# Ten of 32 modulation sums, and the row they are multiplied with, formed in the first stage of a transformer block

## The chip, the cores and the metric

The kernel runs on one core of a Trainium2 chip. Its engines work side by side, each through its own list of instructions in order: PE multiplies matrices, DVE (VectorE) and ACT (ScalarE) work on vectors, POOL (GpSimd) does a little, and SP (SyncE) issues the transfers, which 16 DMA engines carry out. The metric is the time of the program on the device in microseconds, the median of several runs.

## The reference

One layer of a block over 256 tokens of width 1024, in float32. A conditioning vector c modulates it; a mixer with three branches and gates follows, then a mixture of 32 experts:

```python
cond = jax.nn.silu(c)
mod = cond @ w_ada[layer] + b_ada[layer]              # 1024 -> 6 * 1024
sh_m, sc_m, g_m, sh_f, sc_f, g_f = [m[:, None, :] for m in jnp.split(mod, 6, axis=-1)]
h = rms_norm(x, norm_mix[layer]) * (1.0 + sc_m) + sh_m
x = x + g_m * hybrid_mixer(h, ...)    # h @ w_in, then recurrence, two attentions, 3 x 1024 gates, w_branch, w_out
h = rms_norm(x, norm_ffn[layer]) * (1.0 + sc_f) + sh_f
x = x + g_f * moe_ffn(h, ...)         # router, top 4 of 32 experts, 1024 -> 2048 -> 1024 each
```

The first two of the six parts of mod (sc_m, sh_m) are needed at once, to form h. The other four (g_m, sc_f, sh_f, g_f) are needed only after the branches have been merged.

## The kernel before, in words

*First stage* (`branches`, up to the loop over d). h is formed in eight blocks d of 128 columns, and each block is multiplied with its rows of the weights for v, q, k and the window's k and v as soon as it is there. A product in float32 is made of three matmuls (`mm3`): a weight tile is split by ACT into a rounded part `whi` and by DVE into the rest `wlo`, h into `h[0]` (the cast, L273) and `h[1]` (the subtraction, L274). The modulation of h (`ada_rows`) is formed in groups of blocks, {0}, {1}, {2, 3}, {4, 5}, {6, 7}: PE multiplies silu(c) with weight columns (L246), ACT copies the sums (`rd`, L251), PE picks them into columns (L253), DVE adds the bias (`mod`, L255), multiplies with the norm's gain (`A`, L257) and forms `hd` (L268), from which the casts make h.

*The 32 late sums* (`ada`, L207). Columns 16 to 47 of mod are formed on DVE instead: `csb` is a tile with silu(c) in every row (`row_tile`, eight small matmuls with the name silu), and one instruction multiplies a weight tile `wada` of 128 x 1024 (512 KB) with it and sums along the row; a second, tiny one writes the sum. `ada(i)` makes two sums, and i runs from 8 to 23. Before, `ada(8)` and `ada(9)` stand in the loop over the two tiles of `gr`, the rest in the loop over the 12 tiles of the gates, as the list `ADA` says.

*Then* come normalised q and k (`qk_norm`), the bias table of both attentions (`bias_tiles`: a matmul, an addition `relb` (L282), a store `scr` to DRAM by POOL (L284) and three loads `tz` (L288) that spread it over the partitions), the differential attention `diff` (scores L437 on PE, L439 on DVE reading `tz`), the window attention `swa`, the recurrence `lru`, and 12 weight tiles of gates (`proj_ch`), each split in two halves.

*Then* `merge`, `project`, `route`, and the experts (`moe`), whose 400 MB of weights (`w1h`, `w2h`) pass through a ring of buffers (`order`, `slot`, `blocks`); SP issues a load when the buffer's last reader is done.

*Order.* Only the first instructions stand as written. The rest is put in order by a scheduler that may move instructions of one engine past each other where no data forbids it; the order that it makes is fixed in the program. Sums of late calls therefore stand among the instructions of earlier stages.

Of the kernel before, what the change touches and what calls it, by code (L numbers as in the profile page):

```python
# [10 lines left out]
F32 = mybir.dt.float32  # L11
F32R = mybir.dt.float32r
# [8 lines left out]
T, D, NE, FF = 256, 1024, 32, 1024  # L21
# [8 lines left out]
    + [(s, d) for d in range(8) for s in (4, 3)] + [(5, d) for d in range(8)]  # L30


ADA = [[10], [11], [12, 13], [14, 15], [16, 17], [18, 19], [20, 21], [22, 23], [], [], [], []]


C_C, C_NM, C_NF, C_CW, C_CB, C_BA, C_BX, C_LAM = 0, 8, 16, 24, 40, 44, 48, 52
# [8 lines left out]
class Kernel:  # L45
# [148 lines left out]
    def ada_load(self, i, first=False):  # L194
        ws = []
        for j in range(2):
            ws.append(self.p4("wada") if first else self.p4p.tile([128, D], F32, name="wada", tag="wada", bufs=2))
            src = self.a["wad0"][i] if first else self.a["wada"][i - 8]
            self.nc.sync.dma_start(out=ws[j], in_=src[:, j * D:(j + 1) * D])
        return ws  # L200

    def ada(self, i, ws=None):

        nc = self.nc
        for j, w in enumerate(ws or self.ada_load(i)):
            c = 2 * i + j
            nc.vector.tensor_tensor_reduce(out=w, in0=w, in1=self.csb, scale=0.5, scalar=self.col(C_BADA + c),  # L207
                                           op0=ALU.mult, op1=ALU.add, accum_out=self.mod[:, c:c + 1])
# [339 lines left out]
    def mixer(self):  # L548
        nc, tc, a = self.nc, self.tc, self.a
        with ExitStack() as st:  # L550
            self.dram = st.enter_context(tc.tile_pool(name="dram", bufs=1, space=DRAM))
            self.mix = mix = self.pool(st, "mix", 1)
            self.wsp = self.pool(st, "wsp", 3)
            self.h = [self.keep.tile([128, 8, T], F32R, name=f"h{i}", tag=f"h{i}") for i in range(2)]
            with ExitStack() as s3:
                mid = self.pool(s3, "mid", 1)
                br = [[mid.tile([128, 4, T], F32R, name=f"br{n}{i}") for i in range(2)] for n in range(3)]
                gl = [mid.tile([128, 4, T], F32, name=f"gl{b}") for b in range(6)]
                with ExitStack() as s2:
                    self.early = self.pool(s2, "early", 1, "right")  # L560
                    self.mw = self.pool(s2, "mw", 2, "right")
                    self.aw = self.pool(s2, "aw", 2, "right")
                    self.p4p = self.pool(s2, "p4", 9, "right")
                    self.branches(br, gl)
                self.keep2 = self.pool(self.ctx, "keep2", 1, "right")
                wp2 = self.pool(self.ctx, "wp2", 1, "right")
                self.order += [(wp2, f"v{i}", 2) for i in range(3)]
                self.merge(br, gl)
            self.wst = ExitStack()
            wp3 = self.pool(self.wst, "wp3", 1, "right")  # L570
            self.project(st)
            o = {s[1]: s for s in self.order}
            self.order = [(wp3, f"u{i}", 2) for i in range(3)] + [o["v0"], o["v1"], (wp3, "u3", 1)] \
                + [o[t] for t in ("w1", "w2", "w0", "v2")]
            self.half = None
            self.route()

    def branches(self, br, gl):
# [26 lines left out]
        for d in range(8):  # L605
            if d:
                wt = self.load(a["wqkv"][d])
                hi, lo = self.split(wt[:, :1024])
                self.tokens_k(pv, self.h, d, hi[:, :512], lo[:, :512])
                self.tokens_k(pq, self.h, d, hi[:, 512:], lo[:, 512:])  # L610
            g = groups.get(d)
            if g:
                self.ada_rows(g, [self.ada_load(e, first=True) for e in g])
                for e in g:
                    self.h_chunk(gl[e // 4][:, e % 4], e)
            hi, lo = self.split(wt[:, 1024:]) if d else (hi2, lo2)
            self.tokens_k(pk, self.h, d, hi[:, :512], lo[:, :512])
            for t in range(2):
                tt = slice(t * 128, (t + 1) * 128)
                self.mm3(pkv[:, t * 256:(t + 1) * 256], (self.h[0][:, d, tt], self.h[1][:, d, tt]),  # L620
                         (hi[:, 512:], lo[:, 512:]), d + t == 0, d + t == 8)
        dv = self.p4("dv").rearrange("p (t m) -> p t m", t=2)
        for t, p in enumerate(pv):
            nc.scalar.copy(dv[:, t], p)
        self.csb = self.row_tile("silu", self.sc, self.mix)
        xr = self.p4("xr", 4 * (T + 3)).rearrange("p (c m) -> p c m", c=4)
        nc.vector.memset(xr[:, :, 0:3], 0.0)
        nc.scalar.copy(xr[:, 0:2, 3:], self.proj_ch(0))
# [13 lines left out]
        sq = tok4("sqT")  # L642
        for t, p in enumerate(self.proj([self.po(), self.po()], self.h, a["wsq"])):
            self.qk_norm(p, 512, self.gains[:, 1:2], sq, t)
        self.diff(dq, dk, dv, br[1])
        self.lru_prepare()
        gr = tok4("gr")
        for i in range(2):
            nc.scalar.copy(gr[:, 2 * i:2 * i + 2], self.proj_ch(2 + i))
            self.ada(8 + i)  # L650
        self.swa(sq, sk, sv, br[2])
        self.lru(xr, gr, br[0])
        for b in range(6):
            for i in range(2):
                nc.scalar.activation(gl[b][:, 2 * i:2 * i + 2], self.proj_ch(4 + 2 * b + i), AF.Tanh, scale=0.5)
                for j in ADA[2 * b + i]:
                    self.ada(j)
# [604 lines left out]
```

## Time and profile before

| | |
|---|---|
| median of 3 runs | 1236.62 us (1233.0 to 1238.64) |
| profiled execution | 1236.15 us, of it 1234.4 us span from the first to the last instruction |
| PE busy | 1130.4 us (92%) |
| DVE busy | 452.1 us (37%) |
| ACT busy | 253.8 us (21%) |
| moved by DMA | 470.70 MB, 381 GB/s over the span |
| the 32 late sums (L207) | 40.8 us of DVE, 1277 ns each |

A share of the whole span averages over stages with different limits, so it says little of one stage; the stretches do. A matmul's recorded duration overlaps the next one's, and its pace is read from the distance of two starts. The profile puts a time in square brackets where an engine was idle before an instruction, with what ended the idle time.

### The profile page before, as it was taken

Reading aid. Unit: us, or ns where it says so; the run is one execution under the profiler, and the core shown is the slowest. Engines: PE = TensorE matmul, PEld = TensorE weight load, DVE = VectorE, ACT = ScalarE, POOL = GpSimd, SP = SyncE. Lnnn points to the kernel's source line nnn. Section 1 sums busy time; section 2 is a strip of 40 time slices with the busy share of each in tenths; the row PEclk is TensorE's granted clock in tenths of the full one; section 3 lists DMA queues with packets and bytes.
Section 4 is the critical chain, followed back from the end, with each engine's and each line's share of the span. In section 5 each row is a group of like instructions: output and inputs, shape, how many; then the busy total and the mean of one; then the engine's idle time right before and its main releaser. Section 6 shows DMA issues by size and latency. Waiting matters only on the chain.

```text
span 1234.4 us, 13920 instructions
## 1 busy us (share of the span) xinstructions
PE 1130.4 (92%) x5719; PEld 550.9 (45%) x5720; DVE 452.1 (37%) x889; ACT 253.8 (21%) x441; POOL 11.0 (1%) x19
## 2 busy tenths in 40 slices
PE   6998999998988999998989798989897989898987
PEld 4787889985333334332423242324233323333223
DVE  3578878973123231231314032303131222122232
ACT  4475658443101011010101010101000000100100
POOL 0000000000010000000000000000000000000000
PEclk9999999998989999999999999989999999999999
DMA  9678567795999999999999999999999999999996
GB/s 373 246 254 319 181 207 257 307 375 202 425 419 425 425 426 423 427 425 426 423 428 426 425 425 425 429 424 425 425 426 426 424 426 424 428 425 425 425 402 223
DMA packets 54862, 470.70 MB, mean 381 GB/s; under 512 B 6064, under 2 KB 8168, under 8 KB 21256
## 3 DMA queue, kind: packets, MB, share of 16 engines
q1 hardware_dynamic: 53256, 466.93, 92.0%
q0 software_dynamic: 528, 1.72, 0.4%
q10 hardware_dynamic: 1008, 1.09, 0.3%
q8 instruction: 47, 0.77, 0.3%
q14 instruction: 23, 0.19, 0.0%
HBM read 468.65 MB, written 1.07 MB: 381 GB/s over the span
## 4 chain that ended last, share of the span: by engine, by line
PE 59%; DMA 35%; DVE 4%; ACT 1%; issue 1%; SPq 0%; DVEq 0%; ACTq 0%
DMA wt<-w2h 19%; DMA wt<-w1h 14%; PE po L961 11%; PE mm L961 10%; PE ps L981 9%; PE ps L994 4%; PE ps L921 3%; PE mm L125 3%; PE mm L124 3%; PE mm L126 3%; PE po L124 1%; PE po L125 1%; PE po L126 1%; PE ps L888 1%; PE ps L437 1%; DVE wlo L109 1%
## 5 line engine op out<-in xcount | busy, mean ns | idle before, releaser
L961 PE MATMUL po<-wt,xT 128*64 128x512 f32 x992 | 336.4, 601 | 27.3 <-DMA wt<-w1h 27.2
L961 PE MATMUL mm<-wt,xT 128*64 128x512 f32 x992 | 331.9, 596 | 0.0
L981 PE MATMUL ps<-wt,act 128*64 128x512 f32 x992 | 237.6, 621 | 41.3 <-DMA wt<-w2h 34.6
L987 DVE TENSOR_TENSOR y<-ps,gf 64x512 f32<-64x512 f32 x62 | 42.7, 688 | 353.2 <-PE ps L981 352.5
L961 PEld LDWEIGHTS po<-wt,xT 128*64 128x64 f32 x992 | 88.2, 137 | 167.5 <-issue 112.7
L981 PEld LDWEIGHTS ps<-wt,act 128*64 128x64 f32 x992 | 73.2, 142 | 191.1 <-issue 138.1
L961 PEld LDWEIGHTS mm<-wt,xT 128*64 128x64 f32 x992 | 93.2, 137 | 133.0 <-issue 131.3
L891 DVE TENSOR_TENSOR g<-ps,b1t 128x512 f32<-128x512 f32 x31 | 21.4, 692 | 243.4 <-PE ps L888 243.4
L109 DVE TENSOR_TENSOR wlo<-wt,whi 128x1024 fp32r<-128x1024 f32 x72 | 85.5, 1192 | 23.6 <-ACT whi L117 23.2
L117 ACT CAST whi<-wt 128x1024 fp32r<-128x1024 f32 x72 | 73.3, 1022 | 57.3 <-PE mm L125 21.5
L965 ACT COPY hg<-po 128x512 f32<-128x512 f32 x31 | 18.1, 585 | 301.8 <-PE po L961 254.9
L124 PE MATMUL mm<-h,whi 128*128 128x256 f32 x256 | 73.6, 287 | 0.0
L125 PE MATMUL mm<-h,whi 128*128 128x256 f32 x256 | 73.5, 287 | 0.0
L126 PE MATMUL mm<-h,wlo 128*128 128x256 f32 x256 | 73.0, 285 | 0.0
L994 PE MATMUL ps<-y,swT 128*128 128x512 f32 (+1 forms) x128 | 58.2, 606 | 7.2 <-DVE y L987 7.2
L894 ACT ACTIVATE ps<-g 128x512 f32<-128x512 f32 x31 | 18.6, 601 | 220.6 <-DVE g L892 220.6
L996 DVE TENSOR_TENSOR x<-x,ps 128x512 f32<-128x512 f32 x64 | 43.8, 687 | 18.8 <-PE ps L994 18.8
L125 PEld LDWEIGHTS mm<-h,whi 128*128 128x128 f32 x256 | 48.5, 190 | 2.1 <-issue 1.9
L126 PEld LDWEIGHTS mm<-h,wlo 128*128 128x128 f32 x256 | 48.7, 190 | 1.0 <-issue 1.0
L124 PEld LDWEIGHTS mm<-h,whi 128*128 128x128 f32 x256 | 48.6, 190 | 1.0 <-issue 1.0
L924 ACT ACTIVATE xT<-ps,B,A 128x256 f32<-128x256 f32 x32 | 17.4, 564 | 141.4 <-PE ps L921 141.2
L207 DVE CUSTOM_DVE_ANT_0 wada<-wada,silu,cols 128x1024 f32<-128x1024 f32 x32 | 40.8, 1277 | 6.0 <-DMA wada<-wada 6.0
(342 smaller groups left out, 1097.9 us busy)
## 6 DMA issues: line engine op xcount, KB each, us to landing
wt<-w1h SPq DMA_DIRECT2D x93, 2048.0 KB, 29.5
wt<-w2h SPq DMA_DIRECT2D x47, 2048.0 KB, 29.5
wt<-w1h SPq DMA_DIRECT2D x70, 1024.0 KB, 29.5
wt<-w2h SPq DMA_DIRECT2D x33, 1024.0 KB, 31.0
wt<-wch SPq DMA_DIRECT2D x16, 1024.0 KB, 5.8
wada<-wada SPq DMA_DIRECT2D x32, 512.0 KB, 5.3
wada<-wad SPq DMA_DIRECT2D x16, 512.0 KB, 8.2
wt<-wqkv SPq DMA_DIRECT2D x7, 896.0 KB, 9.3
```

Of the source, the lines that this page charges most:

```text
L109: eng.tensor_tensor(lo, x, hi.bitcast(F32), op=ALU.subtract)
L117: self.nc.scalar.copy(hi, w)
L124: nc.tensor.matmul(out, lhs[0], rhs[0], start=start, stop=False)
L125: nc.tensor.matmul(out, lhs[0], rhs[1], start=False, stop=False)
L126: nc.tensor.matmul(out, lhs[1], rhs[0], start=False, stop=stop)
L207: nc.vector.tensor_tensor_reduce(out=w, in0=w, in1=self.csb, scale=0.5, scalar=self.col(C_BADA + c), op0=ALU.mult, op1=ALU.add, accum_out= ...
L921: nc.tensor.matmul(p[:, i * 256:(i + 1) * 256], self.xs[j][:, t, d * 128:(d + 1) * 128], sel[:, t], start=(t + j == 0), stop=(t + j == 2))
L961: nc.tensor.matmul(p[64 * hf:64 * hf + 64], xT[:, k, i * CAP:(i + 1) * CAP], w[:, (2 * j + hf) * 512:(2 * j + hf + 1) * 512], start=(k == ...
L981: nc.tensor.matmul(py[rows[hf]], act[:, (k % 4) * 2 + k // 4, :], w[:, (2 * i + hf) * 512:(2 * i + hf + 1) * 512], start=(k == 0), stop=(k ...
L987: nc.vector.tensor_mul(self.y[r, hf], py[r], self.gf[r, hf * 512:(hf + 1) * 512])
L994: nc.tensor.matmul(p, swT[r, i, t * 128:(t + 1) * 128], self.y[r, hf], start=True, stop=True)
L996: nc.vector.tensor_add(self.x[:, t, s], self.x[:, t, s], p)
```

## The change

`ada(8)` to `ada(12)`, ten of the 32 sums, are called in the loop of the first stage (`EARLY`: after the first projections of blocks 2, 3, 4, 6 and 7), each with tiles of its own. These tiles (`wadm`) take the memory of gate tiles and branch tiles, which are made only later in the program now. The row `csb` that the sums need is formed at block 1 instead of behind the loop. The other 22 sums are spread over 11 of the 12 gate tiles, two to each; none is left with the tiles of `gr`.

```diff
-ADA = [[10], [11], [12, 13], [14, 15], [16, 17], [18, 19], [20, 21], [22, 23], [], [], [], []]
+ADA = [[13], [14], [15], [16], [17], [18], [19], [20], [21], [22], [23], []]
+EARLY = {2: 8, 3: 9, 4: 10, 6: 11, 7: 12}
...
+    def ada_early(self, i):
+        ws = []
+        for j in range(2):
+            n = 2 * (i - 8) + j
+            ws.append(self.mid.tile([128, D], F32, name="wadm", tag=f"gl{2 + n}" if n < 4 else f"br{n // 2 - 2}{n % 2}"))
+            self.nc.sync.dma_start(out=ws[j], in_=self.a["wada"][i - 8][:, j * D:(j + 1) * D])
+        self.ada(i, ws)
...
-                br = [[mid.tile([128, 4, T], F32R, name=f"br{n}{i}") for i in range(2)] for n in range(3)]
-                gl = [mid.tile([128, 4, T], F32, name=f"gl{b}") for b in range(6)]
+                self.mid = mid
+                br = [[None] * 2 for _ in range(3)]
+                gl = [mid.tile([128, 4, T], F32, name=f"gl{b}") for b in range(2)]
...
+            if d == 1:
+                self.csb = self.row_tile("silu", self.sc, self.mix)
+            if d in EARLY:
+                self.ada_early(EARLY[d])
...
-        self.csb = self.row_tile("silu", self.sc, self.mix)
...
+        for n in (1, 2, 0):
+            br[n] = [self.mid.tile([128, 4, T], F32R, name=f"br{n}{i}", tag=f"br{n}{i}") for i in range(2)]
         self.diff(dq, dk, dv, br[1])
...
             nc.scalar.copy(gr[:, 2 * i:2 * i + 2], self.proj_ch(2 + i))
-            self.ada(8 + i)
...
+        gl += [self.mid.tile([128, 4, T], F32, name=f"gl{b}", tag=f"gl{b}") for b in range(2, 6)]
```

The change moves instructions on every engine. Three places matter below. In the changed kernel line numbers are higher by 2 in the first part of the file and by 11 behind the new function: L255 is L266 there, L207 is L218, L109 is L111.

DVE before, at blocks 2 and 3 of the first stage, from mod to h:

```order
L255 SCALAR_TENSOR_TENSOR mod<-ps,bm 128x4
L257 TENSOR_TENSOR A_104<-mod,cols 128x2
L268 TENSOR_SCALAR hd<-gl_86,A_104,mod 128x256 x2
L109 TENSOR_TENSOR wlo<-wt,whi 128x1024
L109 TENSOR_TENSOR wlo<-wt,whi 128x768
L274 TENSOR_TENSOR h_76<-hd,h_75 128x256 x2
```

and at the same place now (a sum is the pair of L218 rows):

```order
L266 SCALAR_TENSOR_TENSOR mod<-ps,bm 128x4
L218 ISA wadm,mod<-wadm,silu,cols 128x1024
L218 ISA mod 128x1
L268 TENSOR_TENSOR A_94<-mod,cols 128x2
L218 ISA wadm,mod<-wadm,silu,cols 128x1024
L218 ISA mod 128x1
L279 TENSOR_SCALAR hd<-gl_80,A_94,mod 128x256 x2
L111 TENSOR_TENSOR wlo<-wt,whi 128x1024
L285 TENSOR_TENSOR h_76<-hd,h_75 128x256 x2
```

Two sums stand between mod and hd now, one on each side of A; the splits of block 2 have gone ahead of mod, and one split of block 3 stands behind hd. At blocks 4 and 5 two sums stand in the same two places.

PE before, at the same blocks, from the pick (L253) to the first projection of block 2 (`mm`):

```order
L253 MATMUL ps<-pick,rd 128x1 x4
L125 MATMUL po<-wlo,h_75 128x512
L126 MATMUL po<-whi,h_76 128x512
L124 MATMUL ps<-whi,h_75 128x256
L125 MATMUL ps<-wlo,h_75 128x256
L126 MATMUL ps<-whi,h_76 128x256
L124 MATMUL ps<-whi,h_75 128x256
L125 MATMUL ps<-wlo,h_75 128x256
L126 MATMUL ps<-whi,h_76 128x256
L124 MATMUL mm<-whi,h_75 128x512 x2
```

and now:

```order
L264 MATMUL ps<-pick,rd 128x1 x4
L128 MATMUL ps<-whi,h_76 128x256
L126 MATMUL ps<-whi,h_75 128x256
L127 MATMUL ps<-wlo,h_75 128x256
L128 MATMUL ps<-whi,h_76 128x256
L126 MATMUL mm<-whi,h_75 128x512
```

Four matmuls of block 1 are left between the pick and block 2, where there were eight.

The third place is DVE around the bias table (`relb`). Before, the addition stands 31 rows ahead of the first score (L439):

```order
L282 TENSOR_TENSOR relb<-ps,relb 12x383
L361 SCALAR_TENSOR_TENSOR sp<-sp 128x4 x2
L207 ISA wada,mod<-wada,silu,cols 128x1024
L207 ISA mod 128x1
L109 TENSOR_TENSOR wlo<-wt,whi 128x1024
```

Now it stands 14 rows ahead of it; the rows up to the last two of these 14, which are the second row of a sum and a split:

```order
L293 TENSOR_TENSOR relb<-ps,relb 12x383
L174 RECIPROCAL rs_993<-rt 128x8
L344 TENSOR_REDUCE ss_1007<-sq 128x8
L348 TENSOR_TENSOR q<-po,rs_993 128x512
L111 TENSOR_TENSOR wlo<-wt,whi 128x1024
L174 RECIPROCAL rs_1009<-rt 128x8
L373 SCALAR_TENSOR_TENSOR sp<-sp 128x4
L218 ISA wada,mod<-wada,silu,cols 128x1024
L218 ISA mod 128x1
L348 TENSOR_TENSOR q<-po,rs_1009 128x512
L375 SCALAR_TENSOR_TENSOR sp<-sp 128x4
L218 ISA wada,mod<-wada,silu,cols 128x1024
```

The bias table has moved from the projection of q, ahead of two tiles, to the tile just before the scores. On PE, 29 projection matmuls of 512 columns and 73 of 256 stood between its matmul and the first score; now 56 of 256 columns stand there.

## Rows read from the trace of the kernel before

**Rows 1.** Stretches: start:end, length, each engine's busy us, clock, DMA share, GB/s.

```profile
20.00:71.00 51.00, 50.28 (x333) 37.72 (x332) 23.65 (x41) 22.55 (x34) 1.37 (x2) 1.00 0.75 280
71.00:271.00 200.00, 195.25 (x1433) 177.93 (x1432) 170.99 (x339) 124.58 (x220) 3.14 (x5) 0.99 0.74 268
320.00:340.00 20.00, 20.00 (x96) 7.24 (x93) 3.34 (x6) 2.96 (x4) 0.00 (x0) 1.00 1.00 422
```

**Rows 2.** Timeline of SP's queue where it resumes after its pause: start, us, instruction.

```profile
304.60 3.76 SPq L92 DMA_DIRECT2D wt<-w2h  x2
```

**Rows 3.** Timeline of PE at blocks 1 and 2 (idle before in brackets).

```profile
28.78 1.07 PE L246 MATMUL ps<-wada,sc 128*32 128x256 f32 x16
...
30.82 0.95 PE L253 MATMUL ps<-pick,rd 128*128 128x1 f32 x8
...
33.10 0.73 PE L124 MATMUL mm<-whi,h 128*128 128x512 f32 x2
34.12 0.73 PE L125 MATMUL mm<-wlo,h 128*128 128x512 f32 x2 [0.29 <-DVE wlo L109]
```

**Rows 4.** Timeline of DVE at the same place.

```profile
31.80 0.16 DVE L255 SCALAR_TENSOR_TENSOR mod<-ps,bm 128x4 f32<-128x4 f32 x1 [5.68 <-PE ps L253]
...
32.20 0.73 DVE L268 TENSOR_SCALAR hd<-gl,A,mod 128x256 f32<-128x256 f32 x2
```

**Rows 5.** Timeline of PE where block 4 begins.

```profile
46.79 0.73 PE L124 MATMUL mm<-whi,h 128*128 128x512 f32 x2
```

**Rows 6.** Timeline of DVE: one sum and the split behind it.

```profile
87.05 1.28 DVE L207 CUSTOM_DVE_ANT_0 wada<-wada,silu,cols 128x1024 f32<-128x1024 f32 x1
...
88.26 1.22 DVE L109 TENSOR_TENSOR wlo<-wt,whi 128x1024 fp32r<-128x1024 f32 x1
```

**Rows 7.** Timeline of DVE and PE at the first attention's start.

```profile
110.12 1.28 DVE L207 CUSTOM_DVE_ANT_0 wada<-wada,silu,cols 128x1024 f32<-128x1024 f32 x1 [2.37 <-DMA wada<-wada]
112.47 0.28 DVE L439 CUSTOM_DVE_ANT_0 s<-ps,tz 128x128 f32<-128x128 f32 x1
115.14 1.28 DVE L207 CUSTOM_DVE_ANT_0 wada<-wada,silu,cols 128x1024 f32<-128x1024 f32 x1 [2.09 <-DMA wada<-wada]
120.25 0.30 PE L447 MATMUL ps<-kst,e 128*128 128x128 f32 x1 [3.60 <-DVE st L466]
```

**Rows 8.** Timelines of PE and POOL: bias matmul, store, loads, scores; landing of the loads.

```profile
90.42 0.81 PE L281 MATMUL ps<-relb 32*12 32x383 f32 x2
92.24 0.72 POOL L284 DMA_DIRECT2D scr<-relb  x1 [25.02 <-DVE sp L361]
99.29 2.31 POOL L288 DMA_DIRECT2D tz<-scr  x3 [6.33 <-DMA scr<-relb]
DMA to landing us min/median/max: 8.1/10.8/13.0
107.87 0.60 PE L341 MATMUL ps<-kst,q 128*128 128x128 f32 x4
108.40 0.92 PE L437 MATMUL ps<-dk,dq 64*128 64x128 f32 x6
```

**Rows 9.** Stretches without PE and behind them (columns as in rows 1).

```profile
116.65:120.25 3.60, 0.00 (x1) 0.03 (x1) 3.56 (x13) 2.51 (x6) 0.00 (x0) 1.00 0.75 263
121.42:124.83 3.41, 3.41 (x13) 2.67 (x13) 2.43 (x8) 1.29 (x5) 0.00 (x0) 0.50 0.74 227
583.70:590.00 6.30, 3.35 (x17) 1.06 (x16) 0.00 (x0) 0.00 (x0) 0.00 (x0) 1.00 1.01 427
```

**Rows 10.** Stretches of the gate stage (PE, its weight loads, DVE, ACT, POOL, clock, DMA).

```profile
200.00:210.00 10.00, 10.00 (x87) 10.00 (x86) 10.00 (x14) 8.25 (x11) 0.00 (x0) 1.00 0.66 220
240.00:250.00 10.00, 10.00 (x86) 10.00 (x85) 8.74 (x11) 3.77 (x4) 0.00 (x0) 1.00 0.68 247
```

**Rows 11.** DMA issues: count, KB each, median us to landing.

```profile
out<-x ACTq DMA_DIRECT2D x2, 256.0 KB, 2.0
wada<-wada SPq DMA_DIRECT2D x32, 512.0 KB, 5.3
```

## The prediction

> **What bounds the kernel now.** Read the stretches first, to see that the program has two parts with different limits. From 320 us to the last microseconds the 16 DMA engines are full (share 1.00, 422 GB/s) while PE, the matrix engine, waits for them; from 20 us to 271 us PE is nearly always busy (50.28 of 51, then 195.25 of 200) and the DMA engines have a quarter of their time to spare [rows 1]. The two parts are joined in SyncE's issue queue: with every weight buffer full it issues nothing more until 304.60 us, when the matmuls of the first expert free one [rows 2]. From there all bytes that are left stream without a pause, so the end of the program moves one for one with the moment at which PE begins the first expert. What counts is therefore what PE loses before that.
>
> PE runs its matmuls in the order written, at some 0.117 us for 256 columns (87 matmuls in 10.00 us between 200 and 210 us [rows 10]) and twice that for 512, in the first stage as in the gate stage. Where it already has this pace, less work on VectorE (DVE) gives nothing back; only waits can be removed or added.
>
> **What is removed, added and moved.** Nothing is removed. The same 32 sums are formed, ten of them and their ten 512 KB loads now in the first stage, and the eight matmuls of the silu row earlier. A sum holds DVE for 1.21 us, from its start at 87.05 to that of the next instruction at 88.26 [rows 6], so 12.1 us of DVE work moves. Left aside as free: the row's matmuls (same count on the same engine), and the room of the tiles (each load has its own tile in the first stage and is read long before the branch that takes its place).
>
> *First stage.* Columns 2 and 3 of h need this chain: PE puts the picked sums into PSUM, DVE makes mod from them, then A, then hd, ScalarE rounds hd into h, and PE can start the next projection. Before, mod starts at 31.80, hd at 32.20 and the first matmul on the new h at 33.10, so 1.30 us from mod to the matmul [rows 3, 4]; meanwhile PE has eight matmuls left, some 1.15 us, and loses about 0.2 us. In the new order two sums stand inside this chain, one behind mod and one behind A. They add 2 x 1.21, less some 0.1 of the gap between dependent instructions that they fill: 2.3 us, so mod to matmul becomes 3.6 us. Behind the pick PE now has only four matmuls of 256 columns, 0.47 us. It waits 3.6 - 0.5 = 3.1 us, 2.9 more than now. Two small terms come with it. The copy rd and its handover take from the end of the modulation matmuls (28.78 + 1.07 = 29.85) to the pick at 30.82, 0.97 us [rows 3, 4], and the new order has 0.70 us of matmuls there: +0.3. The lower half of h then follows a split of 1.2 us on DVE [rows 6] and is ready some 0.6 us after PE asks for it, where PE now loses 0.29 us [rows 3]: +0.3. Sum for this group 3.5 us.
>
> The group of columns 4 and 5 has the same two sums in the same two places. Now PE comes to the next projection at 46.79 without an idle stretch that the row would name [rows 5]; afterwards two matmuls of 256 columns (0.23 us) stand behind the pick, so PE waits 3.6 - 0.2 = 3.4, 3.2 more, and 0.6 for the lower half: 3.8 us. In the third group (columns 6 and 7) the sums stand ahead of mod, while the modulation matmuls still run, or behind h, and cost nothing: PE then has over 7 us of matmuls before it needs the next split. First stage: 3.5 + 3.8 = **7.3 us**.
>
> *The clock.* After an idle stretch of 3.60 us from 116.65 the granted clock of PE fell to 0.50, that is 1.2 GHz, for 3.41 us from 121.42; in the stretch from 583.70 to 590.00, which begins with 2.95 us without PE, it stayed at 1.00 [rows 9]. Of the 11 idle stretches of 2.7 to 3.6 us in this trace, 9 were followed by such a spell. A spell of 3.41 us costs half of itself, 1.7 us, of which some 0.3 falls into the wait for the lower half. Two new waits of 3.1 and 3.4 us at eight chances in ten: 2 x 0.8 x 1.4 = **2.2 us** (bounds 0 and 3.4).
>
> *Start of the first attention.* Here PE waits 3.60 us now, until 120.25. On DVE two sums wait for their loads there, 2.37 us until 110.12 and 2.09 us until 115.14 [rows 7]. With ten sums done, the loads in front of this place are fewer by three, and I take these two waits as gone. But another takes their place. The score instructions read tz, a bias table that goes through DRAM: PE makes it (90.42 + 0.81 = 91.2), GpSimd issues the store at 92.24 and, when this has landed, the loads at 99.29, the first of which takes 8.1 us and lands at 107.4; so 16.2 us from the bias matmul [rows 8]. Now PE reaches the first scores at 108.40, 17.2 us after that matmul, and tz is just there. In the new order only 56 matmuls of 256 columns and two sets of transposes (0.53 us each, 107.87 to 108.40) lie between, 56 x 0.117 + 1.1 = 7.6 us, and I put DVE at its first score 9.4 us after the bias matmul: two sums and two splits are 4.9 us [rows 6], the small instructions between them some 3, and 1.5 go for a split's buffer that PE frees late (an estimate). If tz takes as long as now, DVE stands still for 16.2 - 9.4 = 6.8 us, with every split behind it. If the store takes 2.0 us and the load 5.3, as the nearest quicker rows have it [rows 11], tz is there at 1.05 + 2.0 + 0.5 + 5.3 = 8.9 us and nothing waits. From the first score to PE's next matmul is 7.78 us now (112.47 to 120.25) less the 2.09 of the load: 5.7; in the new order a sum less, a split and two small instructions more, 5.9. PE has work until 16.7 us after the bias matmul (9.1 us from the first score: now 108.40 to 116.65 [rows 8, 9], and then seven matmuls more). So PE waits 16.2 + 5.9 - 16.7 = 5.4 us at worst and nothing at best. The queue is much the same as now at this place, one load of 512 KB less in it; I take tz at 14.5 us, nearer the measured one: a wait of 3.7 us, as now 3.6. This term is **0**, from -5.3 (the wait and the spell of slow clock behind it) to +1.8.
>
> The Trainium skill has a rule for this place: DMA: Bandwidth & Descriptors, section Anatomy of one DMA — SWDGE (gpsimd) path, gives a DMA from GpSimd some 2.0 us and its bytes at 436 GB/s, which would put tz at 1.05 + 2.0 + 0.5 + 3.2 = 6.8 us as an estimate from that page, and the sum at the second case below. The trace does not agree under load: the store, 18 KB, was issued at 92.24 and the loads that wait for it at 99.29.
>
> A short wait for a late q goes away, since q stands earlier against its transposes in the new order; by the trace's short waits at this place I take **-0.7**. Everything behind (window attention, gates, merge, routing) keeps its pace.
>
> **Sum** against the profiled execution, 1236.15 us (span 1234.4 and 1.75 around it; the median of the runs, 1236.62, is 0.5 higher): 7.3 + 2.2 + 0 - 0.7 = +8.8, so 1245.0 us.
>
> **The rivals.**
> *tz in time.* The traffic around the bias table is thinner with three loads less, tz lands at the lower bound, and the wait of 3.60 us with its slow clock disappears: 8.8 - 5.3 = +3.5, 1239.7 us. For it: the two waits for loads are real and go. Against: the store's way took 7.05 us and the first load 8.1 [rows 8] in a queue that stays nearly as full.
>
> *DVE sets the pace of the gates* (the other side). DVE is busy 10.00 of 10.00 us from 200 to 210, and ten sums less there would give back 10 x 1.21 = 12.1 us. That would make 7.3 + 2.2 - 12.1 = -2.6, 1233.6 us, not slower; it decides if the gate stage shortens by more than 9.5 us. Against: from 240 to 250 us DVE is busy 8.74 and PE still does 86 matmuls in 10 us, against 87 [rows 10], so PE is no faster with a freer DVE.
> The Trainium skill, Perfetto Trace Analysis, section Identifying the Most-Contended Engine, would lead here: occupancy is a fair measure for the vector engine, not for matmuls. By that DVE would be the engine to relieve; the trace's matmul count speaks against it.
>
> *Loads late in the first stage.* Ten loads of 512 KB are 5.2 MB, 12.4 us at 422 GB/s; the DMA engines are idle for 0.25 x 51 = 12.8 us between 20 and 71 us [rows 1]. If the projection weights queued behind them came late by half of that, PE would wait some 5 us more: 1250 us. Against: the queue is up to three blocks ahead, and PE's new waits give it time.
>
> **How the numbers follow.** A change of 0.5% is 6.2 us, about what a measurement of this kernel can tell. Forecast 0.60, tz in time 0.18, DVE pace 0.10, late loads 0.12. The forecast's own range is 1241 to 1249, from its clock and tz bounds. The whole range of 1236.5 to 1251 leaves out the third case and little else. Slower by over 0.5% (above 1242.8): three quarters of the forecast, a little of the second case, all of the last, 0.60. Within: 0.34. Faster: only if the first stage costs less than half of what I reckon and the gates gain as well, 0.06.
>
> **What would show it.** In the profile after, two PE waits of 3 to 3.5 us between 30 and 60 us, ended by the cast of h; a granted clock of 0.50 behind one or both; the end of the projections some 8 to 10 us later; a DVE wait for tz at the first scores; DVE below 9 of 10 in the gate stage with unchanged matmul spacing there; the queue's pause ending about 9 us later than 304.6, and nothing changed behind it. I am wrong if the projections end on time, or if the gate stage is shorter by more than a few us.

## The result, and the profile after

| | before | after |
|---|---|---|
| median of 4 runs | 1236.05 us (1233.0 to 1238.64) | 1248.38 us (1245.65 to 1249.21) |
| profiled execution | 1236.15 us, span 1234.4 | 1248.4 us, span 1246.6 |

The ratio is 1.0095, with a 95% interval of 1.0075 to 1.0114: slower, by 3.4 us more than forecast. Line numbers of after are shifted as the section on the change says.

PE's timeline of after, at the first matmul on a new h in the three groups (blocks 2, 4 and 6), and at the first matmul behind all projections:

```profile
38.75 0.79 PE L126 MATMUL mm<-whi,h 128*128 128x512 f32 x1 [2.91 <-ACT h L284]
...
57.69 0.50 PE L126 MATMUL mm<-whi,h 128*128 128x512 f32 x1 [3.15 <-ACT h L284]
...
74.06 0.50 PE L126 MATMUL mm<-whi,h 128*128 128x512 f32 x1 [1.44 <-ACT h L284]
...
83.98 0.28 PE L126 MATMUL mm<-h,whi 128*128 128x256 f32 x1
```

The last of them stood here before:

```profile
72.03 0.36 PE L124 MATMUL mm<-h,whi 128*128 128x256 f32 x1
```

So the first stage ends 11.95 us later. Of this, 1.00 us stands there ahead of anything that the change does on PE: up to the modulation matmuls `ps<-wada,sc` at block 1 PE does the same matmuls in the same order in both kernels, and it reaches them here, before and after:

```profile
20.74 1.07 PE L246 MATMUL ps<-wada,sc 128*32 128x256 f32 x16
...
21.74 1.07 PE L257 MATMUL ps<-wada,sc 128*32 128x256 f32 x16
```

Executions differ at this place whatever the change: two kernels below that leave this part as it was before (e4 and f5) reach it at 21.25 and 22.06 us. From there on the first stage is 10.95 us longer. The first two waits are the forecast ones; that their cause is the chain is seen on DVE, in its timeline of after at blocks 2 and 3, which answers to [rows 4]:

```profile
35.29 0.16 DVE L266 SCALAR_TENSOR_TENSOR mod<-ps,bm 128x4 f32<-128x4 f32 x1 [0.94 <-PE ps L264]
35.37 1.27 DVE L218 CUSTOM_DVE_ANT_0 wadm<-wadm,silu,cols 128x1024 f32<-128x1024 f32 x1
...
36.57 0.15 DVE L268 TENSOR_TENSOR A<-mod,cols 128x2 f32<-128x2 f32 x1
36.65 1.28 DVE L218 CUSTOM_DVE_ANT_0 wadm<-wadm,silu,cols 128x1024 f32<-128x1024 f32 x1
...
37.85 0.73 DVE L279 TENSOR_SCALAR hd<-gl,A,mod 128x256 f32<-128x256 f32 x2
```

From mod to PE's matmul pass 38.75 - 35.29 = 3.46 us, 1.30 before. The third wait was not forecast. ACT's timeline of after shows it: the cast of the next weight tile waits for a matmul of block 5, and the cast of h stands behind it.

```profile
72.65 1.04 ACT L119 CAST whi<-wt 128x1024 fp32r<-128x1024 f32 x1 [2.56 <-PE ps L128]
73.61 0.71 ACT L284 CAST h<-hd 128x256 fp32r<-128x256 f32 x2
```

Before, the same cast waited for PE too, but it could begin early, since all matmuls of block 5 stood ahead of the pick, which began at 59.01:

```profile
59.21 1.04 ACT L117 CAST whi<-wt 128x1024 fp32r<-128x1024 f32 x1 [1.67 <-PE ps L126]
```

In after eight of these matmuls stand behind the pick, which begins at 70.40, and the cast begins when the last of them is done.

Stretches of after (columns as in [rows 1]): the three stretches at half clock, with PE's waits at the first and the last of them, then the DMA-bound part and the gates, which answer to [rows 1, 9, 10].

```profile
35.83:38.74 2.91, 0.00 (x1) 0.00 (x0) 2.91 (x8) 1.49 (x3) 0.00 (x0) 0.87 1.00 406
37.97:44.80 6.83, 6.05 (x14) 4.56 (x15) 4.83 (x9) 1.12 (x3) 0.00 (x0) 0.50 1.02 415
58.45:61.86 3.41, 3.07 (x8) 2.23 (x8) 0.87 (x3) 0.00 (x0) 0.00 (x0) 0.50 0.09 37
127.01:131.31 4.30, 0.01 (x1) 0.04 (x1) 4.30 (x11) 3.17 (x7) 0.00 (x0) 0.86 0.62 191
130.13:140.37 10.24, 9.07 (x35) 7.35 (x36) 6.99 (x22) 2.99 (x9) 0.00 (x0) 0.50 0.77 265
...
340.00:360.00 20.00, 20.00 (x96) 7.89 (x94) 4.71 (x8) 2.96 (x4) 0.00 (x0) 1.00 1.01 422
210.00:220.00 10.00, 10.00 (x87) 10.00 (x86) 9.42 (x11) 9.58 (x15) 0.00 (x0) 1.00 0.45 134
240.00:250.00 10.00, 10.00 (x86) 10.00 (x85) 7.94 (x11) 4.38 (x5) 0.00 (x0) 1.00 1.02 425
```

In the gates DVE is somewhat freer than in [rows 10] (9.42 and 7.94 us of 10) and PE does the same 87 and 86 matmuls. At the first attention the timelines of PE, POOL and DVE of after answer to [rows 7, 8]:

```profile
109.05 0.49 PE L292 MATMUL ps<-relb 32*12 32x383 f32 x1
112.46 0.72 POOL L295 DMA_DIRECT2D scr<-relb  x1 [32.47 <-DVE rs L174]
117.55 0.49 PE L448 MATMUL ps<-dk,dq 64*128 64x128 f32 x4
117.59 1.28 DVE L218 CUSTOM_DVE_ANT_0 wada<-wada,silu,cols 128x1024 f32<-128x1024 f32 x1 [0.61 <-DMA wada<-wada]
117.97 2.32 POOL L299 DMA_DIRECT2D tz<-scr  x3 [4.79 <-PE ps L352]
126.01 0.29 DVE L450 CUSTOM_DVE_ANT_0 s<-ps,tz 128x128 f32<-128x128 f32 x1 [5.99 <-DMA tz<-scr]
131.30 0.44 PE L458 MATMUL ps<-kst,e 128*128 128x128 f32 x1 [4.30 <-DVE e L480]
```

The bias matmul starts 8.5 us ahead of the first score instead of 17.98, DVE's first score, which waits for tz, starts 16.96 us after it, and DVE stands still for 5.99 us. Last, SP's queue, which resumed at 304.60 [rows 2]:

```profile
317.59 0.33 SPq L94 DMA_DIRECT2D wt<-w2h  x1
```

That divides the 12.2 us between the spans: +11.95 up to the end of the projections (1.00 of it ahead of the change); +1.0 from there to SP's resumption (232.57 us before, 233.61 now); -0.8 behind it (929.8 and 929.0 us).

### The profile page after: what moved, and what is told of

Read it like the earlier page. It is cut to its first block, busy times and chain, and to the rows that moved or that the text cites. A ratio compares the mean times of both kernels' runs of the same rounds, so it can differ in the third digit from the quotient of the medians.

```text
span 1246.6 us, 13904 instructions
## 1 busy us (share of the span) xinstructions
PE 1131.0 (91%) x5719; PEld 554.9 (45%) x5720; DVE 453.2 (36%) x889; ACT 253.8 (20%) x441; POOL 11.2 (1%) x19
## 4 chain that ended last, share of the span: by engine, by line
PE 53%; DMA 34%; DVE 2%; issue 1%; ACT 1%; ACTq 0%; SPq 0%; DVEq 0%; POOLq 0%
DMA wt<-w2h 19%; DMA wt<-w1h 14%; PE po L978 11%; PE mm L978 10%; PE ps L998 8%; PE ps L1011 4%; PE ps L938 3%; PE mm L127 3%; PE mm L126 3%; PE mm L128 3%; PE ps L905 1%; PE ps L448 1%; PE po L127 1%; PE po L126 1%; PE po L128 1%; PE ps L967 1%
## 5 line engine op out<-in xcount | busy, mean ns | idle before, releaser
L998 PE MATMUL ps<-wt,act 128*64 128x512 f32 x992 | 233.0, 611 | 43.0 <-DMA wt<-w2h 36.1
L111 DVE TENSOR_TENSOR wlo<-wt,whi 128x1024 fp32r<-128x1024 f32 x72 | 85.7, 1193 | 45.1 <-ACT whi L119 44.5
L1011 PEld LDWEIGHTS ps<-y,swT 128*128 128x128 f32 (+1 forms) x128 | 22.6, 189 | 42.3 <-DVE y L1004 24.5
```

The lines of the kernel that those rows point to most:

```text
L111: eng.tensor_tensor(lo, x, hi.bitcast(F32), op=ALU.subtract)
L998: nc.tensor.matmul(py[rows[hf]], act[:, (k % 4) * 2 + k // 4, :], w[:, (2 * i + hf) * 512:(2 * i + hf + 1) * 512], start=(k == 0), stop=(k ...
L1011: nc.tensor.matmul(p, swT[r, i, t * 128:(t + 1) * 128], self.y[r, hf], start=True, stop=True)
```

## The experiments

Times are medians; ratios are to the kernel before on the same chip, with 95% intervals.

**Where the first stage loses its time.** The first kernel keeps the sums out of the chain by making them read h:

```diff
+BEHIND = {8: 3, 9: 3, 10: 5, 11: 5, 12: 7}
...
+        b = self.col(C_BADA + 2 * i, 2)
+        self.nc.vector.scalar_tensor_tensor(b, self.h[1][:, BEHIND[i], 0:2].bitcast(F32), 0.0, b,
+                                            op0=ALU.mult, op1=ALU.add)
         self.ada(i, ws)
```

> The changed kernel, with each of the five early calls' sums made to wait for h of its group (blocks 3, 5, 7), so that no sum can stand between mod and hd; loads, the silu row and all else are as in the change. Theory (the first stage loses its time because two sums of 1.21 us stand in the chain from mod to h): the two PE waits of 2.91 and 3.15 us that the changed kernel shows at blocks 2 and 4 fall under 0.7 us, the half-clock stretches behind them (6.83 and 3.41 us) go, and the third wait of 1.44 us stays; in all 5.0 + 5.1 = some 10 us less than the changed kernel's 1248, about 1238 to 1240. What is left over the kernel before, 2 to 4 us, is the third wait and the longer slow stretch at the first attention. Rival A (the ten loads or the moved silu row cost the time, not the place of the sums): no change, 1246 to 1249. Rival B (DVE, not the order in it, is too full for the first stage): the waits move to the splits behind h and half of the time comes back, 1243 to 1244.

Measured: 1247.31 us, 1.0075 (1.0056 to 1.0095): next to nothing came back. PE's wait at block 2 fell to 0.76 us, but at blocks 4 and 6 it waits 2.60 and 2.26 us. Its timelines of PE and ACT at blocks 4 and 5:

```profile
51.64 1.05 PE L268 MATMUL ps<-pick,rd 128*128 128x1 f32 x8 [0.76 <-ACT rd L266]
55.29 1.22 PE L127 MATMUL mm<-whi,h 128*128 128x512 f32 x2 [2.60 <-ACT whi L120]
...
53.57 0.72 ACT L288 CAST h<-hd 128x256 fp32r<-128x256 f32 x2 [1.98 <-DVE hd L283]
54.20 2.72 ACT L120 CAST whi<-wt 128x1024 fp32r<-128x1024 f32 x3
```

The sums are out of the chain, but the scheduler has put every matmul of block 3 ahead of the pick, so nothing covers the chain, and the weight cast behind h. The edit changed two things. The next kernel leaves the ten sums out altogether (their columns of mod are set to a constant) and keeps their loads, tiles and the early row:

```diff
-        self.ada(i, ws)
+        self.nc.gpsimd.memset(self.mod[:, 2 * i:2 * i + 2], 0.5)
```

> The changed kernel with the ten early sums left out (columns 16 to 25 of mod are set to a constant by GpSimd), while their ten loads, the tiles and the early silu row stay. Theory (the first stage loses to the sums in the chain): the two waits of 2.91 and 3.15 us are gone or under 1.3 us, the half clock behind them too, 7 to 10 us less than the changed kernel's 1248: 1238 to 1241. Rival (the loads, which make the queue of the first stage 5 MB longer, or the scheduler's order on PE and ACT that comes with them, cost the time): waits of 2 to 3 us stay at the groups, ended by a load, by the cast of a weight tile or by h; 1244 to 1248.

Measured: 1245.63 us, 1.0063 (1.0039 to 1.0087). The rival's number and its waits, 0.76, 2.60 and 2.26 us as in e1: the same order comes out with no early sum at all.

```profile
51.01 1.05 PE L264 MATMUL ps<-pick,rd 128*128 128x1 f32 x8 [0.76 <-ACT rd L262]
54.67 1.22 PE L126 MATMUL mm<-whi,h 128*128 128x512 f32 x2 [2.60 <-ACT whi L119]
```

So the next kernels fix the order by hand and then vary one thing each. g2 adds edges, which fix the order of instructions on one engine and add no wait: four matmuls of `pk` (the product for k) behind the modulation matmuls, the other two and the six of `pkv` (the window's k and v) behind the pick, h behind the next weight cast on ACT and the second weight cast of the block behind h, and the early sums behind the last h on DVE. Three of its edits:

```diff
+                with tc.issue_after(self.row.ins):
+                    self.mm3(pk[0], (self.h[0][:, d, :128], self.h[1][:, d, :128]), (hi[:, :512], lo[:, :512]), False, False)
+                    nc.tensor.matmul(pk[1], self.h[0][:, d, 128:], hi[:, :512], start=False, stop=False)
+                with tc.issue_after(self.picked.ins):
...
+                    for c in self.h_casts:
+                        tc.add_manual_dep(c.ins, self.cast.ins.name, mybir.DependencyInfo(
+                            mybir.DependencyClass.NoSync, mybir.DependencyReason.DATA), reason="cast")
...
+        with self.tc.issue_after(self.last_h.ins):
+            self.ada(i, ws)
```

> The changed kernel with the order of the first stage fixed by hand around each of the three groups as it was before: four matmuls of 512 columns, the pick, and eight matmuls behind it on PE; the cast of the next weight tile ahead of h on ACT; and the early sums queued on DVE behind h of their group. The first experiment had the sums behind h too, but the scheduler then put no matmul between pick and h and the weight cast behind h, and PE waited 2.60 and 2.26 us for that cast instead. Theory (what counts is the chain from pick to h and the matmuls that cover it; the sums, loads and the silu row cost nothing by themselves): no PE wait above 1 us at the three groups but at most the 1.44 of the third, no half clock in the first stage, and 9 to 11 us less than the changed kernel's 1248: 1237 to 1240, with the first attention's wait of some 4 us and its slow stretch still there. Rival (the first stage has no room for ten sums and 5 MB of loads in whatever order: each puts the splits of later blocks back): waits at the splits, 1243 to 1248.

Measured: 1236.81 us, 1.0002 (0.9992 to 1.0011): the change's whole loss is gone, with the same sums, loads and row in the first stage. PE's timeline of g2 at blocks 2 and 4 has no wait to name (nor at block 6), and in the stretch behind it the clock of the whole stage is 1.00:

```profile
36.67 0.50 PE L126 MATMUL mm<-whi,h 128*128 128x512 f32 x1
...
49.76 0.50 PE L126 MATMUL mm<-whi,h 128*128 128x512 f32 x1
```

```profile
20.00:75.13 55.13, 52.97 (x345) 39.97 (x343) 34.29 (x62) 21.33 (x34) 0.22 (x1) 1.00 0.87 339
```

The stage is not quite as short as before: it ends at 75.13, 3.10 us later, of which 1.14 stand at block 1's modulation matmuls already (21.88) and 1.29 are a wait for a weight cast at its end. SP resumes at 306.28, 1.68 us later than before.

Now the sums go back into the chain (edges mod, sum, A, sum, hd, and one that keeps the next split behind hd), and in another kernel the cover is cut (`pk` and the first half of `pkv` ahead of the pick). The edges of h1 are these:

```diff
+            if i in (8, 10):
+                self.behind(x, self.ins_A if j else self.ins_m)
+                for y in self.ins_h if j else [self.ins_A]:
+                    self.behind(y, x)
```

> The kernel of g2_old_order_sums_behind, whose time is that of the kernel before, with one thing put back: at blocks 2, 3 and at blocks 4, 5 two sums stand in the chain again, one between mod and A and one between A and hd. PE keeps its eight matmuls behind the pick, ACT its casts. Theory (each sum in the chain is worth its 1.21 us, less 0.1): PE waits some 2.3 us more at each of the two groups, 2.4 to 2.6 us, so +4.6 us on g2 without a slow clock, and up to 5 us more if half clock follows these waits as it follows those of the changed kernel: 1241 to 1246. Rival (the sums' place is free; the changed kernel lost its time by the scheduler's new order on PE and ACT alone, as the run without sums might suggest): as g2, 1236 to 1239.

> The kernel of g2_old_order_sums_behind with the sums behind h, but only three matmuls of 256 columns (0.35 us) between the pick and the next block instead of eight (1.15 us), at all three groups. Theory (the chain of 1.30 us from mod to the first matmul must be covered by what stands behind the pick): a PE wait of some 1 us at each group, no half clock behind it, +2 to +3 us on g2: 1239 to 1240. Rival (what is ahead of the pick does as well, since rd is copied earlier relative to it): no change, 1236 to 1238.

Measured: h1 1243.74 us, 1.0053 (1.0035 to 1.0071); h2 1239.4 us, 1.0032 (1.0016 to 1.0048). PE's timeline of h1 at blocks 2 and 4, and the stretches of h1 at half clock there:

```profile
38.12 1.22 PE L126 MATMUL mm<-whi,h 128*128 128x512 f32 x2 [2.26 <-ACT h L294]
...
55.93 0.73 PE L126 MATMUL mm<-whi,h 128*128 128x512 f32 x2 [2.21 <-ACT h L294]
```

```profile
36.98:43.80 6.82, 5.67 (x13) 4.46 (x14) 5.99 (x11) 2.56 (x5) 0.00 (x0) 0.50 0.77 290
57.41:60.82 3.41, 3.41 (x10) 2.63 (x10) 2.16 (x3) 0.48 (x1) 0.00 (x0) 0.50 0.49 92
```

PE's timeline of h2 at blocks 2, 4 and 6:

```profile
36.08 0.50 PE L126 MATMUL mm<-whi,h 128*128 128x512 f32 x1 [0.88 <-ACT h L287]
...
49.99 0.50 PE L126 MATMUL mm<-whi,h 128*128 128x512 f32 x1 [0.87 <-ACT h L287]
...
64.73 0.50 PE L126 MATMUL mm<-whi,h 128*128 128x512 f32 x1 [0.87 <-ACT h L287]
```

Both theories held. Two sums in the chain cost 2.2 us at each group, and the same half clock follows as in the changed kernel. The sizes agree only roughly: waits of 4.5 us and up to half of 5.67 + 3.41 make 8.6 to 9.0 us, where the medians of h1 and g2 differ by 6.9. The profiled spans, 1245.6 and 1236.7, differ by 8.9, but h1 also has a longer wait at the first attention (4.03 against 2.93 us), with half clock for 6.83 us there instead of 3.41, and lacks g2's wait of 1.29. Five matmuls less behind the pick cost 0.9 us at each, and no half clock follows: 3 x 0.87 = 2.6 us, as much as the medians of h2 and g2 differ (their profiled spans differ by 0.7). The last part of the change alone, in the kernel before with the same edges for PE and ACT (no run has these edges without the row):

```diff
+            if d == 1:
+                self.csb = self.row_tile("silu", self.sc, self.mix)
...
-        self.csb = self.row_tile("silu", self.sc, self.mix)
```

> The kernel before with its order around the three groups fixed by hand as it was, and with the silu row formed at block 1 instead of behind the loop; no sum is moved. Theory (the row's sixteen matmuls are free in count, but eight of them filled PE's gap at 60.21 while h of blocks 6 and 7 was made, and eight the gap at 71.22 ahead of the first tile behind the projections): 1 to 3 us lost at these two places, 1237 to 1240. Rival (they were no filler, PE only does them earlier): no change within 0.5 us, 1236 to 1237.

Measured: 1237.43 us, 1.0009 (0.9997 to 1.002). Nothing that can be told from zero, though the interval reaches 2.5 us. In its trace the stage takes 50.87 us from block 1's modulation matmuls to the first matmul behind the projections (21.66 to 72.53), 51.29 before, so the theory of a lost filler is not borne out.

**Where the gates gain nothing.** The kernel before without ten sums and their loads:

> The kernel before with ten of its 32 late sums and their ten loads left out altogether (calls 8 to 12; columns 16 to 25 of mod are set to a constant instead), so 12.1 us of DVE work and 5.2 MB are gone from the attention and gate stages and nothing is added anywhere. It is the most that moving these sums out of there can bring. Theory (PE keeps its pace of some 87 matmuls in 10 us there, and DVE has work to spare for it): only what hangs on waits for wada at the first attention can come back, 2.37 + 2.09 us and part of a slow stretch, 0 to 6 us less than before: 1230 to 1236. Rival (DVE sets the pace of the gate stage, 10.00 of 10.00 us busy from 200 to 210 us): 10 to 14 us less, 1222 to 1226.

Measured: 1235.78 us, 1.0 (0.9988 to 1.0012). The rival is excluded: 12.1 us of DVE work less did not give back 10 to 14 us, and PE's matmul count stays as it was with DVE at 8.37 instead of 10.00:

```profile
200.00:210.00 10.00, 10.00 (x88) 10.00 (x87) 8.37 (x9) 9.59 (x12) 0.00 (x0) 1.00 0.59 199
```

That the work is worth nothing at all is not shown: in the profiled execution half clock at the first attention covered 10.23 us, from 119.03, instead of 3.41, which can hide some 3 us (an estimate). DVE's timeline at the first attention also answers another question:

```profile
110.16 1.28 DVE L207 CUSTOM_DVE_ANT_0 wada<-wada,silu,cols 128x1024 f32<-128x1024 f32 x1 [2.29 <-DMA wada<-wada]
...
114.75 1.28 DVE L207 CUSTOM_DVE_ANT_0 wada<-wada,silu,cols 128x1024 f32<-128x1024 f32 x1 [1.74 <-DMA wada<-wada]
```

With ten loads fewer, both waits of [rows 7] are still there, 2.29 and 1.74 for 2.37 and 2.09 us: later sums have come to the same place in the order, and wait for their loads there.

**The first attention.** The bias table is started ahead of the normalisation of q, in the changed kernel (e3), in e1 (e6), in g2 (g4) and in the kernel before (f5):

```diff
         self.attn_gains()
+        self.late_constants()
+        self.bias_tiles()
         for t in range(2):
             self.qk_norm(pq[t], 512, self.gains[:, 0:1], dq, t)
...
-        self.late_constants()
         self.attn_prepare()
-        self.bias_tiles()
```

> The changed kernel, with the bias table (its matmul, addition, store and the three loads) called ahead of the normalisation of q, so that it starts some two tiles earlier; the sums stay where the change put them. Theory (at the first attention the wait is for tz, whose way through DRAM takes some 16 us from the bias matmul and now begins too late): DVE's wait of 5.99 us for tz goes, PE's wait of 4.30 us until the first transposes falls to under 1 us, and the half-clock stretch of 10.24 us with it: 4 to 9 us less than the changed kernel's 1248, about 1240 to 1243 where the two waits in the first stage stay. Rival (the wait is the attention's own chain from score over the row sums to e, 5 to 6 us, whatever tz does): tz is in time and PE still waits some 4 us; no change, 1247 to 1249.

> The changed kernel with both edits: sums behind h, and the bias table ahead of the normalisation of q. Theory: the two causes add up, 10 us from the first stage and 4 to 9 from the first attention, so 1229 to 1235, faster than the kernel before by 0.1 to 0.6%, since the slow stretch of the first attention, which the kernel before has too (3.60 us wait and 3.41 us at half clock), is gone as well. Rival (one wait only moves to the next place: what is gained in the first stage or at the table is lost in the window attention or the gates): 1237 to 1243.

> The kernel of g2_old_order_sums_behind with the bias table started ahead of the normalisation of q as well. Theory (both causes are found and add up): some 8 us less than g2, as the same edit gave between the changed kernel and e3; 1229 to 1233, faster than before by 0.3 to 0.6%. Rival (what the early table gave was only the slow stretch that the late sums had made): no more than before has, 1235 to 1238.

> The kernel before with nothing changed but the bias table started ahead of the normalisation of q. By the trace of before tz is in DRAM's way until 107.4 us and the first score stands at 108.40, so the table is not what is waited for there; the two sums that wait for their loads are. Theory: no change, 1235 to 1238. Rival (the table sets the start of the attention in the kernel before too, so that the gain of e3 owes nothing to the ten sums moved): 1229 to 1232.

Measured: e3 1240.45 us, 1.0032 (1.0022 to 1.0042), as its theory said, 7.9 us less than the changed kernel. Its timelines of DVE and PE have no wait for tz and 0.21 us for e, and in the stretch the clock stays up:

```profile
122.01 0.28 DVE L450 CUSTOM_DVE_ANT_0 s<-ps,tz 128x128 f32<-128x128 f32 x1
...
128.12 0.30 PE L458 MATMUL ps<-kst,e 128*128 128x128 f32 x1 [0.21 <-DVE st L477]
```

```profile
116.00:150.00 34.00, 33.08 (x247) 28.73 (x248) 30.99 (x91) 21.09 (x50) 0.00 (x0) 1.00 0.76 266
```

e6 came to 1245.05 us, 1.0068 (1.005 to 1.0087), outside both expectations: it has the e1 order, with waits of 2.60 and 2.26 us for the weight cast. f5 came to 1238.08 us, 1.0008 (0.9995 to 1.0022): before, tz was not what was waited for. What made the table late in after needn't be the ten sums: in e2, where no sum is moved, it starts 11.28 us ahead of the first score and DVE waits 7.09 us for tz, until 114.68. g4 came to 1234.01 us, 0.9981 (0.997 to 0.9991), faster than before, but by less than expected. Its timelines of DVE and PE and the stretch behind show why: a late sum's load is waited for, q is late by it, and half clock follows.

```profile
101.13 1.28 DVE L219 CUSTOM_DVE_ANT_0 wada<-wada,silu,cols 128x1024 f32<-128x1024 f32 x1 [2.53 <-DMA wada<-wada]
...
109.36 0.66 PE L353 MATMUL ps<-kst,q 128*128 128x128 f32 x4 [1.82 <-DVE q L349]
```

```profile
110.41:117.24 6.83, 6.83 (x30) 5.59 (x29) 4.86 (x16) 3.66 (x8) 0.00 (x0) 0.50 0.79 266
```

So the last kernel, g4 with one edit more, queues the late sums behind the first e on DVE:

```diff
-                for j in ADA[2 * b + i]:
-                    self.ada(j)
+                with self.tc.issue_after(self.first_e.ins):
+                    for j in ADA[2 * b + i]:
+                        self.ada(j)
```

> The kernel of g4_and_bias_early with the 22 late sums queued on DVE behind the first e of the first attention. In g4's trace a late sum waits 2.53 us for its load at 101 us, the last q is late by it, PE waits 1.82 us and runs at half clock for 6.83 us from 110.4. Theory: these go, 2 to 5 us less than g4's 1234: 1229 to 1232, 0.4 to 0.6% faster than before. Rival (DVE is full from there to the end of the window attention, and what it does not do early it must do late): PE waits for splits or scores there instead, 1233 to 1237.

Measured: 1232.63 us, 0.9969 (0.9957 to 0.9981), faster than both kernels, though a little short of its theory's 1229 to 1232; the intervals of g4 and k1 overlap, so the gain over g4 is not clear of the noise. In PE's timeline of k1 no wait for q or e is left at the first attention, and in the stretch from the projections to the merge the clock is full:

```profile
109.15 0.65 PE L353 MATMUL ps<-kst,q 128*128 128x128 f32 x4
...
114.37 0.28 PE L459 MATMUL ps<-kst,e 128*128 128x128 f32 x1
```

```profile
76.00:277.00 201.00, 198.06 (x1451) 179.50 (x1452) 164.40 (x321) 125.34 (x223) 3.14 (x5) 1.00 0.70 254
```

## Why the prediction was right, and where its terms were off

The direction and the mechanism held: the end moves with SP's resumption, and what moved it is what PE lost in the first stage. Two signs came out larger than forecast, the end of the projections (11.95 us later for 8 to 10) and of the queue's pause (12.99 for about 9), and DVE in the gates stayed at 9.42 of 10 us in one stretch, not below 9. That the first stage's waits add up as forecast is partly luck. By its own steps:

*The chain.* Forecast 3.6 us from mod to the matmul and waits of 3.1 and 3.4; measured 3.46, 2.91 and 3.15. h1 shows the two sums' part (2.2 us a group against 2.3), h2 that of the cover (0.9). The prediction was right to count both. But e5 and e1 show that "sums in the chain" is what they cost in this one order: with the sums gone or moved, the order that the scheduler makes costs as much in another place.

*The small terms*, 1.2 us for rd and the lower halves, were too large: the only wait for a lower half that is named in after is 0.34 us, at 59.05.

*The third group*, put at 0, cost 1.44 us. The step considered DVE alone; the wait came by ACT, where h stands behind a weight cast that waits for PE's last matmul of block 5, and eight of that block's matmuls had moved behind the pick. This alone doesn't make the wait: in g2 eight stand there as well, but the cast begins at 60.95, ahead of the pick at 61.39, and PE doesn't wait. Why the cast is late in after and not in g2 was not varied by itself and stays open; that the row's matmuls no longer stand in this gap (as a cover) isn't supported by e2. By size, the 1.44 stands in for the small terms: the named waits of after, 2.91, 3.15, 1.44 and 0.34, less 0.29 and 0.25 before, make 7.3 us, the number forecast from other parts.

*The clock* was mis-sized: 2.2 us forecast, from spells of 3.41 us. Measured were 6.83 and 3.41 us with PE busy for 6.05 and 3.07 of them. In such a spell of after, matmuls of 512 columns start 0.43 us apart (41.55 and 41.98), behind it 0.23 (45.13 and 45.36), so a spell costs 0.45 of its work and not half: 0.45 x 9.12 = 4.1 us. Of the 11.95 us by which the first stage ends later, 1.00 lies ahead of what the change does on PE; the other 10.95 stand against 7.3 + 2.2 = 9.5. The waits' 7.3 and 4.1 make 11.4, 0.5 too many, which was not followed.

*The first attention*, put at 0: the wait for tz came as forecast, nearer its worst case. Counted as in the prediction, from the end of the bias matmul (109.86; the line above shows the first of its two records), DVE had tz after 16.15 us where 14.5 was taken and 16.2 was the bound. The rest of the sum was nearly right: 5.29 us from the first score to PE's matmul for 5.9, and PE's work lasted 17.15 us for 16.7. So PE waited 16.15 + 5.29 - 17.15 = 4.3 us against 3.7, but half clock covered 9.07 us of its work instead of 3.41. The rule of the Trainium skill that was weighed there (DMA: Bandwidth & Descriptors, Anatomy of one DMA — SWDGE (gpsimd) path) gave 6.8 us as an estimate; this trace doesn't agree with it under load, with 16.15 us. Since wait and spell were longer than taken, the rival that has tz in time was priced too low: 5.3 us, where e3 gained 7.9. The two waits for loads are gone in after, as forecast, but for 0.61 us. The reason given fell: with ten loads fewer both are there in e4, and with the ten sums moved DVE waits 1.92 and 1.70 us in e3 and 3.64 us in g2. What decides, as far as k1 shows it, is where the order puts a sum against its load: with the late sums behind the first e no such wait is left. From the end of the projections to SP's resumption the whole came to +1.0 against -0.7, where the longer wait and spell alone make +0.7 and, at 0.45 of 9.07 - 3.41, some +2.5 (an estimate). Some 2.2 us came back: 1.0 in PE's other idle time (6.47 us before, 5.43 after, without the waits of 3.60 and 4.30), with the wait of 0.66 us for q among it, as forecast; the rest was not followed.

*Behind it* nothing changed, as said, but the profiled executions differ by 0.8 us there.

*The rivals.* DVE does not set the pace of the gates: 87 and 86 matmuls in 10 us with DVE freer, and e4. In [rows 10] PE and its weight loads were busy for 10.00 of 10.00 us as well, so busy time alone didn't single out DVE. No late load held PE in the first stage of after: the three waits end by h, and no sum in the chain of blocks 2 to 5 waits for its load.

## What to carry to other kernels

Work moved into idle time of an engine is free only if it stays out of the chains that another engine waits for; look at what stands between the ends of each such chain in the new order, and at how much the waiting engine has left to do meanwhile. Where a scheduler makes the order, taking away a suspected cause changes the order too, so fix the order first and then vary one thing: only so did g2, h1 and h2 separate what e1 and e5 had mixed. And price a stall with the slow clock that may follow: here some 4 us (0.45 of 9.07, an estimate) behind a wait of 4.30.

## What the runs showed that was not expected

Half clock of 6.83 us began in or behind a wait of 2.26 us in h1 and one of 1.82 us in g4, and of some 10.2 us in one of 4.30 us in after and one of 3.08 us in e4; none followed 1.44 us in after, 0.88 us in h2, or 2.15 us ahead of the transposes of q at 116.71 in e3. So a longer wait didn't always mean a longer spell, and the prediction's single length of 3.41 us was too simple.

The way of the bias table through DRAM depended on the moment: from the store's issue to that of the loads behind it 5.51 us in after and 7.05 before [rows 8], but 2.58 us in g4, where it ran at 82 us. Only before does the profile name the store as what ended the loads' wait; in after and g4 it names a matmul and a weight cast, so there the time needn't be the store's.
